# Twenty more weight pairs by seven half-size products in a hybrid mLSTM, GLA and SwiGLU block, with one weight sum made by an accumulating transfer

## The chip, the cores and the metric

The kernel is one program on one core of a Trainium2 chip. Its time is the device time of a launch in microseconds, the median of three runs. The work is shared by five engines with queues of their own, each in order: PE (TensorE, matrix products), ACT (ScalarE), DVE (VectorE), POOL (GpSimd) and SP (SyncE, which here only issues transfers). A queue stands still while its first instruction waits.

## The reference, cut to what matters

```python
for l in range(DEPTH):                       # DEPTH = 1, 512 tokens, 16 meta tokens, D_MODEL = 1024
    xn = rmsnorm(h, norm1_g[l])
    proj = jnp.where(valid, xn @ w_in[l].astype(dt), 0.0).astype(dt)
    (mq, mk, mv, mi, mf, mo, gq, gk, gv, ga, gr, gate_m, gate_g) = split_cols(proj)
    ...
    y_m = hm.reshape(bsz, tp, M_V).astype(dt)      # chunked mLSTM, 4 heads, head norm, gate sigmoid(mo)
    ...
    y_g = hg.reshape(bsz, tp, G_V).astype(dt)      # chunked gated linear attention (GLA), 4 heads, gate silu(gr)
    merged = (jax.nn.sigmoid(gate_m) * (y_m @ w_branch_m[l].astype(dt))
              + jax.nn.sigmoid(gate_g) * (y_g @ w_branch_g[l].astype(dt)))
    h = h + merged @ w_out[l].astype(dt)
    hn = rmsnorm(h, norm2_g[l])
    ff = jax.nn.silu(hn @ w_ff_gate[l].astype(dt)) * (hn @ w_ff_up[l].astype(dt))
    h = h + ff @ w_ff_down[l].astype(dt)
out = rmsnorm(h, final_g)
```

Everything is float32. The two mixers read the same normed input, so their projections (mq to gate_g) are products of one 1024-row activation with many 128-column blocks of weights.

## The kernel before

Activations lie transposed: a tile has 128 features on the partitions and up to 528 tokens (16 meta tokens and 512 real ones) along the columns. A **unit** is one block of weights of 128 output features, a tile `raw` of 128x1024 that holds eight 128x128 blocks, one for each k of the 1024 input features. Full float32 accuracy is had from rounded products: each operand is split in a high part (rounded to float32r) and a low part (the rest), and `mm3` (L194 to L200) issues three matmuls per k: high by high (L198), high by low (L199), low by high (L200). The weights are split on the chip: `whi` (L164) is a cast on ACT, `wlo` (L169) a subtraction on DVE.

A unit over the real tokens only (`unit_real`) is 8 k of three matmuls with 512 columns; one over all tokens (`unit_all`) is 8 k of three matmuls for each of two halves of 264 columns. The units run one after the other in a fixed order (`ORDER`): gates; four mLSTM heads (mq, mk, mv, mv, mo, mo); four GLA heads (gq, gk, gv, gv, gr, gr) with the merge gates gm and the branch products bm of the mLSTM output put in after heads 1 and 2; then gg 0 to 7, bg 0 to 7 (branch of the GLA output), out 0 to 7; 22 pairs fg, fu of the feed-forward layer; 22 units of its down projection. Below, mv6 is the unit ("mv", 6), and so on.

The last 17 of the 22 feed-forward pairs take a cheaper form already. Instead of two products over k = 0 to 7 with 512 columns, a **pair** is seven products over four k with 256 columns (a Strassen scheme): 7 x 4 x 3 = 84 matmuls, L1054 to L1056. The products are named p7, q1, p3, q6, p4, p2, q5; each takes one 128x512 sum of quarters of the two weight tiles and one sum of parts of the activations. The activation sums are made once (`operands`); the weight sums for each pair by four additions of 128x512 on DVE (L1014, L1015, L1018, L1021), and then split by ACT and DVE.

What sets the order around the change: while a unit u runs, `ahead` (L184) asks at k = 0 for the transfer of unit u + 5 (`load_raw`, SP's queue, four `raw` tiles), and at k = 2 and 4 splits the weights of unit u + 3. After each k, `tick` (L136) moves every side generator one step: evacuation of the products (`evac_all`, `evac_real`, `gates_of`), the convolution on mq and mk (`conv`, L451 and L454 on DVE), and, one head after the other, the mixers (`mlstm`, `gla`), whose rows are interleaved in this way into PE's, DVE's and ACT's queues. At the end of a head `head_out` norms its output and splits it into high and low parts (L570 on ACT, L572 on DVE) for the branch units.

## Time and profile before

| | |
|---|---|
| median of 3 runs | 956.32 us (956.04 to 956.37) |
| the profiled execution | 956.21 us, its span in the trace 954.2 us, mean granted TensorE clock 0.997 |
| transfers | 89.40 MB, mean 94 GB/s |

The span is the time from the first to the last instruction in the trace; about 2 us of the execution lie outside it. "Busy" counts an engine's instructions, not the waits between them. PE's matmuls overlap, so the time that one costs is the distance from its start to the start of the next, not its recorded duration; the same holds in a smaller measure on DVE and ACT, where a following instruction starts before the recorded end of the one ahead.

### The profile page before, as it was taken

The page shows a single profiled execution, that of the slowest core. Times are in us where ns is not written, and L with a number is a line of the kernel's source. Part 1 is how long each engine was busy: PE and PEld are TensorE (multiplying, and loading weights), DVE is VectorE, ACT ScalarE, POOL GpSimd, SP SyncE. Part 2 cuts the span into 40 slices and gives each one's busy share as a digit, 9 for nine tenths or more (in the row PEclk, how much of TensorE's full clock was granted, in tenths as well). Part 3 has the DMA queues.
Part 4 walks back from the last instruction along what each step waited for, and adds up shares of the span by engine and source line. Part 5 has one row for each costly group of instructions (what it writes and reads, how often), then busy time and mean ns, then how long its engine had stood idle before and what let it go on. Part 6 is the DMA issues. An engine that isn't in the chain of part 4 may idle for free.

```text
span 954.2 us, 13802 instructions
## 1 busy us (share of the span) xinstructions
PE 935.1 (98%) x5687; PEld 832.8 (87%) x5687; DVE 601.2 (63%) x876; ACT 467.6 (49%) x778; POOL 11.7 (1%) x30
## 2 busy tenths in 40 slices
PE   6999999999999999999999999999999999999995
PEld 6988989898988898889888888879999999888885
DVE  6898877674854543452354555798888887842323
ACT  7457667675552544262442234445555555732321
POOL 0000000000000000000000000010000000000000
PEclk9999999999999999999999999999999999999998
DMA  7322221212223232233223343223334233422202
GB/s 262 110 89 69 87 89 45 89 50 84 71 70 94 81 88 85 66 111 89 67 67 110 111 136 129 67 89 105 117 90 129 93 111 112 133 90 87 89 1 88
DMA packets 27294, 89.40 MB, mean 94 GB/s; under 512 B 3040, under 2 KB 5088, under 8 KB 27232
## 3 DMA queue, kind: packets, MB, share of 16 engines
q1 hardware_dynamic: 26144, 87.49, 29.2%
q10 hardware_dynamic: 1088, 1.05, 0.3%
q8 instruction: 44, 0.72, 0.3%
q14 instruction: 18, 0.15, 0.1%
HBM read 86.43 MB, written 2.10 MB: 93 GB/s over the span
## 4 chain that ended last, share of the span: by engine, by line
PE 88%; DVE 8%; ACT 2%; issue 1%; DMA 1%; SPq 0%; DVEq 0%
PE b L198 21%; PE b L200 21%; PE b L199 21%; PE b L1055 6%; PE b L1056 6%; PE b L1054 6%; DVE wlo L169 1%; PE b L767 1%; ACT t L116 1%; PE b L769 1%; PE b L746 1%; PE b L653 1%; PE b L486 1%; PE b L654 1%; DMA t<-xT 1%
## 5 line engine op out<-in xcount | busy, mean ns | idle before, releaser
L198 PE MATMUL b<-t,whi 128*128 128x512 f32 (+2 forms) x1222 | 434.9, 356 | 6.9 <-ACT t L116 6.9
L200 PE MATMUL b<-t,wlo 128*128 128x512 f32 (+2 forms) x1222 | 427.4, 350 | 0.7 <-DVE wlo L169 0.7
L199 PE MATMUL b<-t,whi 128*128 128x512 f32 (+2 forms) x1222 | 427.0, 349 | 0.7 <-DVE t L272 0.7
L198 PEld LDWEIGHTS b<-t,whi 128*128 128x128 f32 x1222 | 231.2, 189 | 36.2 <-ACT t L116 6.8
L200 PEld LDWEIGHTS b<-t,wlo 128*128 128x128 f32 x1222 | 230.8, 189 | 32.6 <-DVE wlo L169 1.1
L199 PEld LDWEIGHTS b<-t,whi 128*128 128x128 f32 x1222 | 231.3, 189 | 30.4 <-DVE t L272 1.0
L169 DVE TENSOR_TENSOR wlo<-raw,whi 128x1024 fp32r<-128x1024 f32 x138 | 168.2, 1223 | 96.0 <-ACT whi L164 95.9
L164 ACT CAST whi<-raw 128x1024 fp32r<-128x1024 f32 x138 | 142.9, 1047 | 17.7 <-issue 7.1
L1056 PE MATMUL b<-t,wlo 128*128 128x256 f32 x408 | 114.6, 281 | 0.0
L1055 PE MATMUL b<-t,whi 128*128 128x256 f32 x408 | 114.5, 281 | 0.0
L1054 PE MATMUL b<-t,whi 128*128 128x256 f32 x408 | 114.2, 280 | 0.0
L1054 PEld LDWEIGHTS b<-t,whi 128*128 128x128 f32 x408 | 76.9, 188 | 0.1
L1055 PEld LDWEIGHTS b<-t,whi 128*128 128x128 f32 x408 | 76.8, 188 | 0.1
L1056 PEld LDWEIGHTS b<-t,wlo 128*128 128x128 f32 x408 | 76.7, 188 | 0.0
L116 ACT ACTIVATE t<-t 128x512 f32<-128x512 f32 (+3 forms) x78 | 43.7, 579 | 45.0 <-DVE t L553 19.5
L116 ACT ACTIVATE t<-b 128x512 f32<-128x512 f32 (+1 forms) x65 | 33.5, 541 | 55.6 <-PE b L200 23.2
L169 DVE TENSOR_TENSOR wlo<-ws,whi 128x1024 fp32r<-128x1024 f32 x34 | 41.5, 1221 | 7.4 <-ACT whi L164 7.4
L116 ACT ACTIVATE t<-f 128x256 f32<-128x256 f32 (+1 forms) x24 | 11.6, 482 | 67.2 <-DVE f L1205 67.2
L1070 ACT COPY t<-b 128x256 f32<-128x256 f32 x51 | 19.0, 373 | 45.6 <-PE b L1056 45.6
L1205 DVE TENSOR_TENSOR f<-f,b 128x512 f32<-128x512 f32 (+1 forms) x9 | 5.7, 629 | 53.9 <-PE b L200 53.9
L164 ACT CAST whi<-ws 128x1024 fp32r<-128x1024 f32 x34 | 35.8, 1052 | 6.3 <-DVE ws L1021 3.5
L791 DVE TENSOR_TENSOR t<-b,t 128x512 f32<-128x512 f32 x16 | 11.1, 691 | 30.8 <-PE b L200 30.8
(200 smaller groups left out, 958.0 us busy)
## 6 DMA issues: line engine op xcount, KB each, us to landing
raw<-wst SPq DMA_DIRECT2D x155, 512.0 KB, 3.5
t<-xT SPq DMA_DIRECT2D x8, 264.0 KB, 5.6
t<-xT SPq DMA_DIRECT2D x8, 256.0 KB, 3.7
out<-t SPq DMA_DIRECT2D x4, 256.0 KB, 2.3
out<-t ACTq DMA_DIRECT2D x4, 256.0 KB, 2.5
cn<-con SPq DMA_DIRECT2D x1, 516.0 KB, 7.3
pr<-par SPq DMA_DIRECT2D x1, 320.0 KB, 7.1
pr<-par SPq DMA_DIRECT2D x1, 44.0 KB, 1.9
```

Source lines behind the costliest of these rows:

```text
L116: S.activation(o, i, func, **kw)
L164: S.copy(t, src)
L169: V.tensor_tensor(t, src, hi.bitcast(F32), ALU.subtract)
L198: T.matmul(o, w_h, ah[:, c0:c1], start=first, stop=False)
L199: T.matmul(o, w_h, al[:, c0:c1], start=False, stop=False)
L200: T.matmul(o, w_l, ah[:, c0:c1], start=False, stop=last)
L486: T.transpose(pb[:, c * P:(c + 1) * P], f[:, c * CH:(c + 1) * CH], ident)
L791: V.tensor_tensor(t, ps, t, ALU.mult)
L1054: T.matmul(o, h, xh_[k], start=start and k == 0, stop=False, skip_group_check=not start)
L1055: T.matmul(o, h, xl_[k], start=False, stop=False, skip_group_check=not start)
L1056: T.matmul(o, l, xh_[k], start=False, stop=k == 3, skip_group_check=not start)
L1070: s7=lambda: S.copy(s[:, lo], bz), s1=lambda: S.copy(s[:, hi], bx), s2=lambda: S.copy(r[:, lo], bx),
```

## The change

Twenty more pairs are run by seven half-size products: (gq, gk) and both gv and both gr of each GLA head, and gm and gg two by two. The pairs that need all tokens (gq with gk, gv) have 272 columns in each product, the others 256. The new generator `mixed_x` makes the seven sets of activation operands from the normed input while mv6, mv7, mo6 and mo7 run. It has 32 steps, and before the first gm pair the program issues all that is left of it (`while len(X.w["p4"][1]) < 4: tick()`). The order of the units changes (`JOBS`): after the mLSTM heads come gm0-1, gm2-3, GLA head 0, gm4-5, gm6-7, bm 0 to 7, the other heads with their parts interleaved, gg 0 to 7 between and behind them, bg 0 to 7.

Every pair, the 17 old ones too, now gets two of its four weight sums by accumulating transfers that POOL issues: one onto half of the second unit's `raw` tile (L182), one onto half of a tile `wf` that SP first fills (L210, L211), two pairs ahead of its use. DVE makes the other two (`s2` at L226, `s4` at L238). Weights are split two items ahead instead of three units, from four buffers instead of five. Several additions and multiplications move from DVE to ACT: the first tap of the convolution (L451 before, an activation now), two squares, a minimum in the GLA decay and a scaling of the GLA state. `head_out` no longer splits its result: `parts` does (L829 on ACT, L830 on DVE), just ahead of the first branch unit (bm0, bg0); only two tiles of the GLA output are split under gg6.

```diff
 NSTD = 5
...
+def job_list():
+
+    one = lambda *a: [(x,) for x in a]
+    o = one(("gates", 0))
     for h in range(H):
-        o += m(h)
-    for h in range(H):
-        o += g(h)
-        if h in (1, 2):
-            for i in range(4 * h - 4, 4 * h):
-                o += [("gm", i)] if i % 2 == 0 else [("gm", i), ("bm", i - 1), ("bm", i)]
-    o += [("gg", i) for i in range(8)] + [("bg", i) for i in range(8)]
+        o += one(("mq", h), ("mk", h), ("mv", 2 * h), ("mv", 2 * h + 1), ("mo", 2 * h), ("mo", 2 * h + 1))
+    two = lambda n, i: [((n, 2 * i), (n, 2 * i + 1))]
+    g = lambda h: [(("gq", h), ("gk", h))] + two("gv", h) + two("gr", h)
+    bm = lambda i: one(("bm", 2 * i), ("bm", 2 * i + 1))
+    o += two("gm", 0) + two("gm", 1) + g(0) + two("gm", 2) + two("gm", 3)
+    for i in range(4):
+        o += bm(i)
+    q, v, r = ([g(h)[i] for h in range(H)] for i in range(3))
+    o += [q[1], v[1], q[2], r[1], v[2], q[3], r[2], v[3]] + two("gg", 0) + [r[3]]
+    for i in range(1, 4):
+        o += two("gg", i)
+    for i in range(8):
+        o += one(("bg", i))
...
+            if v - 1 in MIXED:
+                G.dma_start(lr(r, 0), lr(wst[v - 1], 0), accum_op=ALU.add)
...
-        t = wpool.tile([P, D], F32R, tag="wlo", name=nm("wlo"), bufs=5)
+        t = wpool.tile([P, D], F32R, tag="wlo", name=nm("wlo"), bufs=4)
...
+            st.f = wpool.tile([P, D], F32, tag="wf", name=nm("wf"), bufs=2)
+            nc.sync.dma_start(lr(st.f, 1), lr(wst[u + 1], 0))
+            G.dma_start(lr(st.f, 1), lr(wst[u + 1], 1), accum_op=ALU.add)
...
+    def s2(u):
+        b = raws.pop(u + 1)
+        V.tensor_tensor(lr(mixw[u].f, 0), lr(b, 0), lr(b, 1), ALU.add)
...
+    PLAIN = {"s": [(split_hi, 2), (split_lo, 4)], "e": [(e_hi, 1), (e_lo, 3), (s2, 4)],
+             "a": [(a_hi, 1), (a_lo, 3), (f_hi, 4), (s4, 5)]}
+    FIRST = {"s": [(split_hi, ("q1", 2)), (split_lo, ("p3", 1))],
+             "e": [(e_hi, ("q1", 2)), (e_lo, ("p3", 1)), (s2, ("q6", 1))]}
+    SECOND = {"s": [(split_hi, ("p2", 0)), (split_lo, ("p2", 2))],
+              "a": [(a_hi, ("p2", 0)), (a_lo, ("p2", 2)), (f_hi, ("q5", 0)), (s4, ("q5", 2))],
+              "e": [(e_hi, ("p2", 0)), (e_lo, ("p2", 2)), (s2, ("q5", 2))]}
...
+        load_raw(u + 5)
+        while ready[0] < min(item_ix[0] + 2, len(ITEMS)):
+            kind, v = ITEMS[ready[0]]
+            ready[0] += 1
+            for f, at in tables.pop(0)[kind]:
+                steps.setdefault(at, []).append(lambda f=f, v=v: f(v))
...
+        seven(bz, w, x, "p7", True, hook, *cols)
+        seven(bx, w, x, "q1", True, hook, *cols)
+        if "p3" in pend:
+            pend.pop("p3")(hook)
+        else:
+            for k in range(4):
+                hook("p3", k)
+        seven(bx, w, x, "q6", False, hook, *cols)
+        seven(bz, w, x, "p4", False, hook, *cols)
+        seven(by, w, x, "p2", True, hook, *cols)
...
+        h, l = X.h, X.l
+        c1, c2 = slice(0, HA), slice(256, NT)
+        X.w = {n: ([], []) for n in SEVEN}
...
+        for k in (0, 2):
+            for j in range(2):
+                t = tt(F32R, 2 * HA)
+                for i in range(2):
+                    c = slice(i * HA, (i + 1) * HA)
+                    S.copy(t[:, c], (h, l)[j][k + i][:, c1])
+                    X.w["q1"][j].append(t[:, c])
+                yield 1
+            t1, t3 = tt(n=2 * HA), tt(n=2 * HA)
+            for j in range(2):
+                b1, b2 = tt(), tt()
+                u1, u3 = three(t1)[:, j], three(t3)[:, j]
+                V.tensor_tensor(b1, h[k + j].bitcast(F32), l[k + j].bitcast(F32), ALU.add)
+                yield 1
+                V.tensor_tensor(b2, h[k + 4 + j].bitcast(F32), l[k + 4 + j].bitcast(F32), ALU.add)
+                yield 1
+                V.tensor_tensor(u1, b1[:, c1], b1[:, c2], ALU.subtract)
+                V.tensor_tensor(u3, b2[:, c2], b1[:, c2], ALU.subtract)
+                yield 1
+                two("q5", u1, j)
+                yield 1
+                two("p7", u3, j)
+                V.tensor_tensor(u1, u1, b2[:, c2], ALU.add)
+                yield 1
+                two("q6", u1, j, True)
+                V.tensor_tensor(u3, u1, b2[:, c1], ALU.subtract)
+                yield 1
+                two("p4", u3, j)
...
+    def parts(y, k):
+
+        if k < 6 and y is ym:
+            hi = hpool[0].tile([P, NS], F32R, tag="h", name=nm("h"))
+        else:
+            hi = tt(F32R, NS)
+        lo = tt(F32R, NS)
+        S.copy(hi, y[k])
+        V.tensor_tensor(lo, y[k], hi.bitcast(F32), ALU.subtract)
+        y[k] = hi, lo
...
+    def joined(y, k):
+        while y[k] is None:
+            tick()
+        if not isinstance(y[k], tuple):
+            parts(y, k)
+
+    def branch_unit(name, y):
+        for k in range(KT):
+            joined(y, k)
+        return unit_real(name, [a[0] for a in y], [a[1] for a in y])
...
+            if what == "gm" and i == 0:
+                while len(X.w["p4"][1]) < 4:
+                    tick()
...
+            if i == 3:
+                run(mixed_x())
...
-            V.tensor_tensor(lr(st.s, 0), lr(st.b, 0), lr(st.a, 0), ALU.add)
-            V.tensor_tensor(lr(st.r, 0), lr(st.b, 0), lr(st.b, 1), ALU.add)
```

How the rows on the engines move, at three places. In DVE's queue of the kernel before, this stands around the weight split that is issued while mv6 runs, there that of mo7 (L617, L630 and L634 are the state chain of mLSTM head 3, L567 and L572 the output of head 2, L454 the convolution of head 3, L169 a weight split):

```order
L617 TENSOR_TENSOR t_1840<-b_1836,t_1840 128x400
L567 TENSOR_TENSOR t_1151<-t_1151,t_1687 128x512
L454 SCALAR_TENSOR_TENSOR t_1877<-t_1864,pr,t_1877 128x528
L169 TENSOR_TENSOR wlo_1916<-raw_1684,whi_1887 128x1024
L630 TENSOR_TENSOR wl_1784<-t_1840,wh_1783 128x400
L634 TENSOR_TENSOR t_1789<-t_1789,t_1840 128x400
L572 TENSOR_TENSOR t_1919<-t_1151,t_1918 128x512
L567 TENSOR_TENSOR t_1160<-t_1160,t_1687 128x512
L617 TENSOR_TENSOR t_1896<-b_1892,t_1896 128x272
L630 TENSOR_TENSOR wl_1784<-t_1896,wh_1783 128x272
```

In DVE's queue of the changed kernel, ahead of and behind the weight split issued while mv6 runs, now that of mo6 (L885, L898 and L902 are that state chain, L818 the output of head 2, L704 the convolution, L192 a weight split; L540 to L569 are `mixed_x`: sums and differences of activation tiles, and L569 the low part of each operand set, whose high part ACT has cast):

```order
L540 TENSOR_TENSOR t_1903<-t_566,t_567 128x528
L885 TENSOR_TENSOR t_1843<-b_1839,t_1843 128x400
L818 TENSOR_TENSOR t_1159<-t_1159,t_1688 128x512
L704 SCALAR_TENSOR_TENSOR t_1883<-t_1868,pr,t_1883 128x528
L542 TENSOR_TENSOR t_1904<-t_863,t_864 128x528
L192 TENSOR_TENSOR wlo_1931<-raw_1595,whi_1896 128x1024
L818 TENSOR_TENSOR t_1168<-t_1168,t_1688 128x512
L544 TENSOR_TENSOR t_1901<-t_1903 128x272
L545 TENSOR_TENSOR t_1902<-t_1904,t_1903 128x272
L569 TENSOR_TENSOR t_1943<-t_1901,t_1942 128x272
L898 TENSOR_TENSOR wl_1787<-t_1843,wh_1786 128x400
L902 TENSOR_TENSOR t_1792<-t_1792,t_1843 128x400
```

Of ten rows before, none made operands; of these twelve, five do (L540 to L569), and `mixed_x` has 40 such rows in all between the start of mv6 and the start of gm0-1.

In DVE's queue before, the end of the last GLA head's output, ahead of bg0 (L562, L563, L567 norm it, L572 splits its two tiles, L169 splits weights, L791 takes up the product of bg0):

```order
L562 TENSOR_SCALAR t_4629<-t_4629 128x512
L563 TENSOR_TENSOR t_4628<-t_4628,t_4629 128x512
L567 TENSOR_TENSOR t_4470<-t_4470,t_4628 128x512
L572 TENSOR_TENSOR t_4733<-t_4470,t_4732 128x512
L567 TENSOR_TENSOR t_4471<-t_4471,t_4628 128x512
L572 TENSOR_TENSOR t_4754<-t_4471,t_4753 128x512
L169 TENSOR_TENSOR wlo_4768<-raw_4659,whi_4759 128x1024
L169 TENSOR_TENSOR wlo_4799<-raw_4698,whi_4791 128x1024
L169 TENSOR_TENSOR wlo_4834<-raw_4742,whi_4826 128x1024
L791 TENSOR_TENSOR t_4565<-b_4810,t_4565 128x512
L793 TENSOR_TENSOR t_4565<-t_4565,t_3208 128x512
```

In DVE's queue of the changed kernel, at the end of the last gg pair and ahead of bg0 (L404 evacuates that pair, L830 splits tiles of the output, L803, L811, L812 and L818 norm the last head):

```order
L404 TENSOR_TENSOR t_5647<-b_5646,t_5649 128x256
L830 TENSOR_TENSOR t_5785<-h_4904,t_5784 128x512
L830 TENSOR_TENSOR t_5789<-h_4916,t_5788 128x512
L830 TENSOR_TENSOR t_5793<-h_5393,t_5792 128x512
L830 TENSOR_TENSOR t_5797<-h_5405,t_5796 128x512
L803 TENSOR_SCALAR t_5800<-b_5775 128x512
L811 SCALAR_TENSOR_TENSOR t_5659<-t_5659,t_5800 128x512
L812 SCALAR_TENSOR_TENSOR t_5658<-t_5659,t_5658 128x512
L818 TENSOR_TENSOR h_5808<-t_5158,t_5658 128x512
L830 TENSOR_TENSOR t_5811<-h_5808,t_5810 128x512
L818 TENSOR_TENSOR h_5814<-t_5159,t_5658 128x512
L830 TENSOR_TENSOR t_5817<-h_5814,t_5816 128x512
```

The split of the last two tiles stood three weight splits ahead of bg0's product; now nothing of another kind stands between it and the branch unit, and four splits of earlier heads stand ahead of the norm.

In POOL's queue before, between the last clearing of convolution edges (L444) and the products for the first feed-forward units (L949), nothing stood but two clears:

```order
L444 MEMSET t_1349 128x3
L444 MEMSET t_1768 128x3
L444 MEMSET t_1864 128x3
L674 MEMSET t_2191 128x512
L674 MEMSET t_2193 128x512
L949 ISA
L949 TENSOR_TENSOR t_5540<-t_5539,t_5540 128x512
```

In POOL's queue of the changed kernel, from the first accumulating transfer onto a `raw` tile on (L182 onto a `raw` tile, L211 onto `wf`, L853 the gate selector of a head, L695 clearing edges):

```order
L182 DMA raw_1858<-wst 128x512
L695 MEMSET t_1868 128x3
L182 DMA raw_2089<-wst 128x512
L853 CAST sel_2233<-cn 128x256
L182 DMA raw_2279<-wst 128x512
L211 DMA wf_2308<-wst 128x512
L182 DMA raw_2450<-wst 128x512
L211 DMA wf_2480<-wst 128x512
L182 DMA raw_2613<-wst 128x512
```

74 accumulating transfers are new in this queue, two for each of 37 pairs.

More of the change, by code (lines that the diff above doesn't have):

```diff
@@ L954, in hybrid_block @@
     xw = {}
+    hx = [[fpool.tile([P, 2, NS], F32, tag="hx", name=nm("hx"), bufs=2) for _ in range(2)] for _ in range(1)][0]
     def operands():
@@ L1190, in block @@
             held[u] = splits.pop(u)
+            down_steps["now"] = begin(("down", u - first))[1]
         mm3(o, held[u], flat % KT, fsp[k][0], fsp[k][1], c0, c1, k == 0, k == FT - 1)
         if prefetch:
-            ahead(u, flat % KT)
+            for f in down_steps["now"].get(flat % KT, ()):
+                f()
         tick()
```

536 lines of the change are left out of this document (299 added, 237 removed).

## The prediction

> **What bounds the kernel now.** I read the page's busy times first, then the chain that ended last, then what PE waited for.
>
> ```profile
> span 954.2 us, 13802 instructions
> ...
> PE 935.1 (98%) x5687; PEld 832.8 (87%) x5687; DVE 601.2 (63%) x876; ACT 467.6 (49%) x778; POOL 11.7 (1%) x30
> ...
> PE 88%; DVE 8%; ACT 2%; issue 1%; DMA 1%; SPq 0%; DVEq 0%
> ```
>
> ```profile
> PE b L198 <- ACT t L116: 6.9, 1, 6.9
> PE b L610 <- DVE t L495: 1.1, 1, 1.1
> PE b L1231 <- ACT t L116: 1.0, 1, 1.0
> ```
>
> PE is busy for 98% of the span and makes up 88% of the chain. Its longest wait is the first 6.9 us; the other two are about 1 us. So what PE executes is the time, as long as DVE and ACT keep ahead of it. The change cuts PE's work and gives DVE more, so I need PE's saving and then the places where DVE falls behind.
>
> **PE's saving.** Recorded durations overlap, so I take distances from start to start in a gapless row of matmuls.
>
> ```profile
> 23.26 0.28 PE L199 MATMUL b<-t,whi 128*128 128x264 f32 x1
> ...
> 24.84 0.28 PE L200 MATMUL b<-t,wlo 128*128 128x264 f32 x1
> ```
>
> ```profile
> 178.20 0.29 PE L652 MATMUL b<-wh,t 128*128 128x272 f32 x1
> ...
> 178.58 0.23 PE L652 MATMUL b<-wh,t 128*128 128x144 f32 x1
> ```
>
> ```profile
> 300.36 0.39 PE L199 MATMUL b<-t,whi 128*128 128x512 f32 x1
> ...
> 301.52 0.40 PE L198 MATMUL b<-t,whi 128*128 128x512 f32 x1
> ```
>
> With 264 columns: 13 steps in 1.58 us, 0.1215 each. With 272: three in 0.38, 0.127; scaled from 264 it would be 0.125, I take 0.126. With 512: five in 1.16, 0.232. For 256 the stretch of the old pairs serves, 651 to 815 us (next fence): 164.0 us for 1391 matmuls, 0.118.
>
> ```profile
> 8.00:24.50 16.50, 16.34 (x111) 16.22 (x112) 14.96 (x19) 14.51 (x24) 1.09 (x2) 1.00 0.67 266
> ...
> 651.00:815.00 164.00, 164.00 (x1391) 163.96 (x1390) 138.37 (x196) 95.00 (x168) 1.61 (x1) 1.00 0.35 107
> ```
>
> Removed: 28 units over real tokens (4 gq, 8 gr, 8 gm, 8 gg) x 24 = 672 matmuls of 512, 155.9 us; 12 over all tokens (4 gk, 8 gv) x 48 = 576 of 264, 70.0 us. Added: 12 pairs x 84 = 1008 of 256, 118.9 us; 8 pairs x 84 = 672 of 272, 84.7 us. Net: 225.9 - 203.6 = **22.3 us less** (21.7 with 0.127, 23 with 0.125). Bounded by PE alone, the profiled execution of 956.2 us would come to 933.9.
>
> **What DVE gets, and where.** These rows show what DVE instructions cost back to back, which is some 0.08 us less than their recorded time.
>
> ```profile
> 163.08 0.77 DVE L454 SCALAR_TENSOR_TENSOR t<-t,pr,t 128x528 f32<-128x528 f32 x1
> 163.75 0.57 DVE L617 TENSOR_TENSOR t<-b,t 128x400 f32<-128x400 f32 x1
> 164.24 0.69 DVE L567 TENSOR_TENSOR t<-t,t 128x512 f32<-128x512 f32 x1
> ...
> 171.84 0.43 DVE L634 TENSOR_TENSOR t<-t,t 128x272 f32<-128x272 f32 x1
> 172.19 0.69 DVE L572 TENSOR_TENSOR t<-t,t 128x512 fp32r<-128x512 f32 x1
> 172.80 0.69 DVE L470 TENSOR_TENSOR t<-t,t 128x512 fp32r<-128x512 f32 x1
> 173.40 0.30 DVE L617 TENSOR_TENSOR t<-b,t 128x144 f32<-128x144 f32 x1
> 173.62 0.70 DVE L470 TENSOR_TENSOR t<-t,t 128x528 fp32r<-128x528 f32 x1
> 174.23 0.30 DVE L630 TENSOR_TENSOR wl<-t,wh 128x144 fp32r<-128x144 f32 x1
> ...
> 174.67 1.22 DVE L169 TENSOR_TENSOR wlo<-raw,whi 128x1024 fp32r<-128x1024 f32 x1
> 175.81 0.17 DVE L617 TENSOR_TENSOR t<-b,t 128x16 f32<-128x16 f32 x1
> ```
>
> So: 1024 columns 1.13, 528 0.61 (scalar-tensor-tensor 0.67), 512 0.60, 400 0.49, 272 0.36, 144 0.22, 16 0.09.
>
> The steady pair is fine. It needs three weight splits (3.4), one low part, two sums (three of 512, 1.8) and four evacuations of 256 to 272 (1.4): 6.6 us of DVE beside 9.9 to 10.6 us of PE. The 17 old pairs lose two sums each, 1.2 us of DVE, and gain nothing: PE is gapless there, 164.00 of 164.00.
>
> The heavy place is **mixed_x under mv6, mv7, mo6, mo7**. Its own 40 DVE instructions are 8 of 528 and 32 of 272, 8 x 0.61 + 32 x 0.37 (four are scalar-tensor-tensor) = 16.6 us. Counting DVE's queue in its new order from the first row behind mv6's first matmul (a convolution tap) up to the low weights that the pair gm0-1 needs for q6: 76 instructions, 5 of 1024, 12 of 528 (three of them taps), 15 of 512, 35 of 272, 3 each of 400, 144 and 16, together 37.6 us. PE's own work from mv6's first matmul to that product is 33.9 us. Up to the same product of (gq0, gk0) it is 117 instructions, 60.3 us, against 56.0 us of PE. So DVE's work exceeds PE's by 4.3 us; and since PE cannot start q6 before it, that excess is a stall. After this the next pairs leave room (one pair on, in gv0, it is 71 against 71).
>
> Two things come on top. The first of those DVE rows cannot run at mv6's start: ACT must copy both halves of mk3 (0.375 each) and make the first tap, which is now an activation of 528 (0.64).
>
> ```profile
> L326 ACT COPY t<-b 128x264 f32<-128x264 f32 x38 | 13.1, 375 | 24.3 <-PE b L200 24.3
> L116 ACT ACTIVATE t<-t 128x528 f32<-128x528 f32 x21 | 12.7, 636 | 4.4 <-DVE t L454 4.3
> ```
>
> That is 1.4 us, or 2.5 with one weight cast between, which I take. And DVE waits for ACT inside: every operand set is cast on ACT before DVE can make its low part. In the same stretch before, 158 to 188 us, such waits are these:
>
> ```profile
> 158.00:188.00 30.00, 30.00 (x196) 27.36 (x195) 22.67 (x39) 18.39 (x37) 1.05 (x2) 1.00 0.23 79
> ```
>
> ```profile
> L495 DVE TENSOR_TENSOR t<-b,t 128x512 fp32r<-128x512 f32 x2 | 1.4, 692 | 3.0 <-ACT t L490 3.0
> ...
> L630 DVE TENSOR_TENSOR wl<-t,wh 128x272 fp32r<-128x272 f32 x1 | 0.4, 443 | 2.2 <-ACT wh L621 2.2
> ```
>
> DVE idles 7.3 of 30 us there, without being late. With a full queue part of it is filled: I take 7% of 60 us, 4.2. The stall is 4.3 + 2.5 + 4.2 = **11 us**, between 4 (the excess alone) and 17 (ACT as slow as in the row, 9 us of waits).
>
> **The ends of the mixers.** Before, the last GLA head was split three units ahead of bg0. Now, as DVE's queue shows, the last head's norm stands behind four splits. From the end of the gg6 pair: those four end some 1.5 us later (4 x 0.60, begun when the pair's evacuation at q5 is done); then L803 0.6, three activations on ACT, two scalar-tensor-tensor 0.67 each, the product 0.6, the cast, the low part 0.6.
>
> ```profile
> L116 ACT ACTIVATE t<-t 128x512 f32<-128x512 f32 x34 | 21.1, 626 | 32.0 <-DVE t L553 19.5 <-DVE t L944 7.1 <-DVE t L454 3.3
> ```
>
> With 0.6 for each on ACT, k = 6 is ready 7.4 us after the pair's end, k = 7 at 9.4. PE comes to k = 6 at 6 x 0.70 + 1.4 (the p3 still owed) = 5.6 us, and would end the unit at 7.0; it ends near 9.9, and eight handings from engine to engine add about half a microsecond: **3.5 us** (2 to 6). At bm0 eight splits stand just ahead, at 0.60 each against 0.70 of PE per k; only the first is late: **1 us** (0 to 2). The rest of GLA's rows, now closer together: **1 us** (0 to 3). The early stretch gets taps on ACT and may lose half of the 1.1 us at L610: **-0.7**.
>
> **The transfers.** Each pair adds three of 128x512, 0.79 MB; 29 MB in all. The fence above shows 266 GB/s in the first stretch and 107 under the old pairs, so there is room. A plain load lands in 3.5 us:
>
> ```profile
> raw<-wst SPq DMA_DIRECT2D x155, 512.0 KB, 3.5
> ```
>
> No accumulating transfer, and none from POOL, is in this trace. A `raw` tile is asked for more than a pair (some 12 us) before its split, so up to 8 us for the accumulation cost nothing. I take nothing, between 0 and the case below. The Trainium skill ("DMA: Bandwidth & Descriptors", Anatomy of one DMA) gives 2.0 us plus bytes over 436e3 for a transfer issued by GpSimd, an estimate of 2.6 us for 256 KB; no run here shows it, and the sum would stay as it is. What stands behind a waiting accumulation in POOL's queue are other accumulations, a head's selector and, in the feed-forward part, its products for the standard units.
>
> **Sum.** 956.2 - 22.3 + 11 + 3.5 + 1 + 1 - 0.7 = **949.7 us** for the profiled execution, which lies 0.1 under the median.
>
> **The rivals.** (1) PE stays the bound: DVE's rows with no bond to PE run ahead of where they are issued, the stretch costs 2 us instead of 11, the ends 1: about 936. For it speaks that DVE is at 63%; against it the excess of 4.3 us in the count, which no order can hide.
>
> (2) A cold clock. At the start PE ran at half pace after its first idle time:
>
> ```profile
> 8.15 0.59 PE L199 MATMUL b<-t,whi 128*128 128x264 f32 x1 [0.71 <-DVE t L272]
> ...
> 13.38 0.39 PE L198 MATMUL b<-t,whi 128*128 128x264 f32 x1
> 13.60 0.29 PE L199 MATMUL b<-t,whi 128*128 128x264 f32 x1
> 13.73 0.28 PE L200 MATMUL b<-t,wlo 128*128 128x264 f32 x1
> ```
>
> Steps of 0.22 (13.38 to 13.60) up to 13.6, then 0.12: 5.4 us at about half pace, 2.4 lost. If the stall at gm0-1 comes in one piece and another such follows, that price is paid twice: 954.5. No wait in the middle of this trace is over 1.3 us, so it is neither shown nor excluded. The Trainium skill ("TensorE: Matmul & The Clock Gate", Part 1) says that the clock falls to half after an idle window of about 3.4 us and returns after about as long of sustained work; by that rule this rival decides whenever a single wait passes 3.4 us, and the slow start agrees with it in kind, though its 5.4 us are longer.
>
> (3) Slower: the exchange between DVE and ACT in mixed_x. There are 16 casts whose low part stands next in DVE's queue. If each costs 1 us of waiting (as in the two rows above, 1.5 and 2.2 each), the waits are 16 us instead of 4.2 and the total 961.5. It turns slower than before at 10.7 us of waits.
>
> (4) Slower by transfers: an accumulation of over 8 us comes late in each of 37 pairs; at 9 us, 37 us are lost, some 987. Nothing in the trace speaks for it.
>
> **How the numbers follow.** Forecast 949.7 (943 to 954): 0.52. PE bound: 0.17. Cold clock: 0.12. Exchange: 0.14. Transfers: 0.05. A measurement tells about 0.2% from no change, so the bounds are 954.4 and 958.2. Faster: 0.50 + 0.17 + half of the cold clock = 0.73. Same: the other half, 0.02 of the forecast and 0.02 of the exchange, 0.10. Slower: 0.17. The range 934 to 962 leaves out about 0.06 below and 0.12 above.
>
> **What would show it.** PE's matmuls of 256 and 272 columns at 0.118 and 0.126 apart; PE's waits by the list: one group of about 11 us between mv6 and the second pair, ended by DVE rows of mixed_x or a weight split; one of 3.5 us in bg0, ended by the split L830 or L829; none in the old pairs. The prediction is wrong if PE waits for a transfer, if those waits are missing, or if steps of 0.22 show up behind a wait.

## The result and the profile after

The changed kernel takes **986.3 us** (median of four runs, 985.17 to 988.49), the kernel before 956.35 us beside it (four runs, 956.04 to 956.56): a ratio of 1.0316 with an interval of 1.0298 to 1.0334. The forecast was 949.7 us with a range up to 962. The profiled execution took 985.17 us, its span 983.4, at a mean granted clock of 0.979 (0.997 before).

The page of the changed kernel: span, busy times, the granted clock in 40 slices of 24.6 us, and the chain that ended last by engine.

```profile
span 983.4 us, 15554 instructions
...
PE 925.5 (94%) x6119; PEld 848.8 (86%) x6119; DVE 651.0 (66%) x970; ACT 551.6 (56%) x959; POOL 78.5 (8%) x107
...
PEclk9999999879999999999997999999999999999998
...
PE 78%; DVE 11%; ACT 9%; issue 2%; DMA 0%; SPq 0%; DVEq 0%; ACTq 0%
```

PE's share of the chain fell from 88% to 78%, and DVE and ACT took it, not a transfer. The clock has a dent in three slices inside (172 to 221 and 516 to 541 us), those of PE's longest waits; the dent in the last slice was there before. PE's waits in the changed kernel (what PE executes, what ended the wait; us in all, times, longest):

```profile
PE b L340 <- ACT t L402: 9.0, 2, 8.4
PE b L300 <- DVE wlo L192: 7.5, 4, 3.6
PE b L340 <- ACT t L400: 7.4, 5, 4.4
PE b L298 <- ACT t L132: 6.7, 1, 6.7
PE b L736 <- ACT t L579: 6.4, 1, 6.4
PE b L340 <- ACT t L568: 4.4, 1, 4.4
```

The 6.7 is the start, as before. The others are new, and most of them end at ACT, where the prediction looked at DVE.

To see where the time went I worked through all of PE's matmul starts. A distance from one start to the next that exceeds its kind's spacing (0.232 for 512 columns, 0.1215 for 264, 0.126 for 272, 0.118 for 256) by more than 0.45 us counts as a wait, with its excess; smaller excesses over 0.05 us count as slow matmuls, added up in slices of 5 us where they pass 0.5.

| place (us of the changed span) | waits | slow matmuls | together | prediction |
|---|---|---|---|---|
| mv6 to gq0 and what follows, 174 to 260 | 20.7 | 6.7 | 27.4 | 11 |
| bg0, 516 to 530 | 8.6 | 1.9 | 10.5 | 3.5 |
| early units, 46 to 65 | 4.2 | 0.9 | 5.1 | -0.7 |
| standard feed-forward units, 644 to 660 | 6.3 | 1.4 | 7.7 | 0 |
| the rest (301 to 512, and 682) | 4.3 | 0 | 4.3 | 2 |

Together 55.0 us, against 2.9 in the middle of the kernel before (2.1 at 55 to 72 us, 0.85 at 634): 52.1 more. The spans differ by 29.2 us (983.4 - 954.2), so what is neither wait nor slow matmul fell by 52.1 - 29.2 = 22.9 us. The count of matmuls at the same spacings (672 fewer of 512 columns, 576 fewer of 264, 1008 more of 256, 672 more of 272) gives 22.3. So the saving is there, and new waits take it back more than twice. Of the 10.9 us of slow matmuls 9.4 stand behind the five waits of 3.8 us and more; the 0.9 at 60 us and the 0.6 at 190 us stand where the granted clock is 1.00, so they are not the clock's doing.

Where nothing waits the change does what it says. One window of the changed kernel under the old pairs (busy us and instructions of PE, PEld, DVE, ACT, POOL; granted clock; share of the DMA engines; GB/s), and the one over mixed_x:

```profile
690.00:850.00 160.00, 160.00 (x1348) 159.74 (x1347) 116.36 (x163) 91.30 (x163) 24.38 (x28) 1.00 0.74 178
158.00:217.00 59.00, 42.67 (x249) 37.54 (x248) 45.06 (x86) 38.77 (x84) 3.97 (x6) 0.87 0.28 68
```

Under the old pairs PE is gapless with the DMA engines busy 0.74 of the time. Over mixed_x PE is busy for 42.67 of 59 us; the kernel before has 59.00 in the same window, with 44.16 us of DVE.

### The profile page after: what moved, and what is told of

It reads as the page before. It is cut to its first block, busy times and chain, and to the rows that moved or that the text cites. A ratio compares the mean times of both kernels' runs of the same rounds, so it can differ in the third digit from the quotient of the medians.

```text
span 983.4 us, 15554 instructions
## 1 busy us (share of the span) xinstructions
PE 925.5 (94%) x6119; PEld 848.8 (86%) x6119; DVE 651.0 (66%) x970; ACT 551.6 (56%) x959; POOL 78.5 (8%) x107
## 4 chain that ended last, share of the span: by engine, by line
PE 78%; DVE 11%; ACT 9%; issue 2%; DMA 0%; SPq 0%; DVEq 0%; ACTq 0%
PE b L298 13%; PE b L300 13%; PE b L299 13%; PE b L340 11%; PE b L341 11%; PE b L342 11%; ACT t L132 4%; DVE wlo L192 2%; ACT whi L187 1%; PE b L1037 1%; ACT L132 1%; ACT L130 1%; PE b L1039 1%; DVE t L830 1%; PE b L736 1%
## 5 line engine op out<-in xcount | busy, mean ns | idle before, releaser
L299 PE MATMUL b<-t,whi 128*128 128x512 f32 (+2 forms) x806 | 284.6, 353 | 1.0 <-DVE t L467 0.7
L298 PE MATMUL b<-t,whi 128*128 128x512 f32 (+2 forms) x758 | 269.2, 355 | 8.6 <-ACT t L132 6.7
L300 PE MATMUL b<-t,wlo 128*128 128x512 f32 (+2 forms) x758 | 266.2, 351 | 7.5 <-DVE wlo L192 7.5
L340 PE MATMUL b<-t,whi 128*128 128x256 f32 (+1 forms) x888 | 258.3, 291 | 14.3 <-ACT t L400 7.4
L341 PE MATMUL b<-t,whi 128*128 128x256 f32 (+1 forms) x888 | 252.4, 284 | 0.7 <-DVE t L569 0.7
L342 PE MATMUL b<-t,wlo 128*128 128x256 f32 (+1 forms) x888 | 252.1, 284 | 0.0
L192 DVE TENSOR_TENSOR wlo<-raw,whi 128x1024 fp32r<-128x1024 f32 x155 | 189.6, 1227 | 54.0 <-ACT whi L187 53.9
L132 ACT ACTIVATE t<-t 128x512 f32<-128x512 f32 (+4 forms) x118 | 67.2, 589 | 26.9 <-DVE t L646 6.8
L182 POOL DMA_DIRECT2D raw<-wst x37 | 32.1, 867 | 411.0 <-DMA wf<-wst 95.0
L187 ACT CAST whi<-wf 128x1024 fp32r<-128x1024 f32 x37 | 38.9, 1051 | 24.0 <-PE b L341 16.5
L340 PE MATMUL b<-t,wgh 128*128 128x256 f32 (+1 forms) x148 | 42.6, 288 | 9.0 <-ACT t L402 9.0
L192 DVE TENSOR_TENSOR wlo<-wf,whi 128x1024 fp32r<-128x1024 f32 x37 | 45.1, 1219 | 0.0
L341 PE MATMUL b<-t,wgh 128*128 128x256 f32 (+1 forms) x148 | 42.4, 286 | 0.0
L342 PE MATMUL b<-t,wgl 128*128 128x256 f32 (+1 forms) x148 | 42.4, 286 | 0.0
```

The costliest lines, as they stand in the source:

```text
L132: S.activation(o, i, func, **kw)
L182: G.dma_start(lr(r, 0), lr(wst[v - 1], 0), accum_op=ALU.add)
L187: S.copy(t, src)
L192: V.tensor_tensor(t, src, hi.bitcast(F32), ALU.subtract)
L298: T.matmul(o, w_h, ah[:, c0:c1], start=first, stop=False)
L299: T.matmul(o, w_h, al[:, c0:c1], start=False, stop=False)
```

## The experiments

Fifteen kernels were run, each beside the kernel before, whose medians lay between 956.2 and 956.4 us. The numbers given are medians of three to five runs (ten for the last version), with the interval of the ratio where the verdict hangs on it. The line numbers in a profile are those of that kernel and shift by a few.

### The lead of the weight splits

The waits at 46 to 55 us and 644 to 660 us lie in units that the change does not touch, but for their weights' split, now two items ahead. In the first kernel that lead is three again wherever four standard units follow each other.

```diff
-        tables = [PLAIN] if len(names) == 1 else [FIRST, SECOND]
+        tables = [PLAIN, PLAIN] if len(names) == 1 else [FIRST, SECOND]
+        far = 3 if all(len(x) == 1 for x in JOBS[j:j + 4]) else 2
...
-        while ready[0] < min(item_ix[0] + 2, len(ITEMS)):
+        while ready[0] < min(item_ix[0] + far, len(ITEMS)):
```

> Weights of single units are split three units ahead again where the next three are single units too; the pairs stay at two items. Theory: the waits at 46 to 55 us (4.2 us) and at 644 to 652 us (6.3 us), with the half-speed matmuls behind them (2.3 us), come from the shorter lead, since DVE and ACT are held up there by other chains that the kernel before has too. They go: 973 to 976 us. Rival, DVE has too much work there: the waits stay, 984 to 987. The waits between mv6 and the first pairs and the one in bg0 stay in both.

Measured: 976.79 us, 9.5 less. Both groups of waits are gone but for 0.9 us at 653.8; three others (0.85, 1.65 and 1.65) appear between 67 and 102 us.

The counterpart shortens the lead in the kernel before, of the single units ahead of the pairs, and changes nothing else.

```diff
-        if not SW0 <= u + 3 < SW1:
+        n = 3 if u >= SW1 else 2
+        if not SW0 <= u + n < SW1:
...
-                split_hi(u + 3)
+                split_hi(u + n)
...
-                split_lo(u + 3)
+                split_lo(u + n)
```

> The kernel before, with the weights of single units ahead of the pairs split two units ahead and not three. Theory: the lead of three is what hides the gate rows at 40 to 60 us and the operands of the feed-forward pairs at 600 to 645 us; without it PE waits there as in the changed kernel, 4 and 6 us and some slow matmuls: 964 to 969 us. Rival: the changed kernel's waits there come from what it moved to ACT: 956 to 958.

Measured: 968.66 us, a ratio of 1.0126 (1.0109 to 1.0143), 12.4 us slower than before. PE's waits in that kernel:

```profile
PE b L201 <- DVE wlo L169: 7.1, 3, 3.6
PE b L199 <- ACT t L116: 6.8, 1, 6.8
PE b L199 <- ACT whi L164: 1.9, 2, 1.3
```

They are 1.42 and 2.18 us at 52 to 56 us, then 1.56, 0.85 and 3.79 at 626 to 638, the sizes that the changed kernel has (1.44 and 2.19, then 1.62, 0.85 and 3.79). So the lead alone makes them; neither pairs nor transfers are needed. Why the first group comes there, ACT's timeline of the changed kernel shows (start, us, instruction, in brackets its wait):

```profile
50.67 0.63 ACT L132 ACTIVATE t<-t 32x512 fp32r<-32x512 f32 x1 [6.78 <-DVE t L646]
51.86 0.62 ACT L656 CAST t<-t 32x512 fp32r<-32x512 f32 x1 [0.55 <-DVE t L653]
52.51 0.62 ACT L658 COPY t<-t 32x512 f32<-32x512 f32 x1
53.15 1.04 ACT L187 CAST whi<-raw 128x1024 fp32r<-128x1024 f32 x1
```

ACT waits 6.78 us for the gate rows on DVE, and the weight cast stands behind. The kernel before has the same wait, of 6.80 us at 50.39, and PE does not notice: the weights in question were split one unit earlier. In the second group DVE is full: it is busy for 13.45 of the 13.6 us from 642.6 to 656.2, and the low parts of the weights stand in its queue among the operand sums of the old pairs (L1265 to L1296). The lead is what covers such chains and such a crowd.

### bg0: a copy behind the last head's norm

PE's longest new wait ends at L402, a copy of one quarter of the last gg pair (s5). It is issued after k = 0 of bg0, behind everything that makes bg0's operands. ACT and PE of the changed kernel there:

```profile
515.86 1.28 ACT L130 ACT_TABLE_LOAD   x1
518.39 1.95 ACT L132 ACTIVATE t<-t 128x512 f32<-128x512 f32 x3 [1.25 <-DVE t L803]
522.55 0.62 ACT L829 CAST t<-h 128x512 fp32r<-128x512 f32 x1 [2.21 <-DVE h L818]
524.53 0.62 ACT L829 CAST t<-h 128x512 fp32r<-128x512 f32 x1 [1.36 <-DVE h L818]
525.05 0.36 ACT L402 COPY t<-b 128x256 f32<-128x256 f32 x1
```

```profile
516.69 0.40 PE L300 MATMUL b<-t,wlo 128*128 128x512 f32 x1
525.47 0.58 PE L340 MATMUL b<-t,wgh 128*128 128x256 f32 x1 [8.38 <-ACT t L402]
525.85 0.42 PE L341 MATMUL b<-t,wgh 128*128 128x256 f32 x1
526.07 0.42 PE L342 MATMUL b<-t,wgl 128*128 128x256 f32 x1
...
529.05 0.59 PE L300 MATMUL b<-t,wlo 128*128 128x512 f32 x1
529.48 0.39 PE L298 MATMUL b<-t,whi 128*128 128x512 f32 x1
529.71 0.40 PE L299 MATMUL b<-t,whi 128*128 128x512 f32 x1
```

The pair's owed product p3 (wgh) accumulates into the bank that L402 reads, so after k = 2 PE stands there, not at k = 6. In the second kernel the copy is issued ahead of the two last tiles' chain.

```diff
         for k in range(KT):
+            if k == 6:
+                left("s5")
             joined(y, k)
```

> In the first branch unit of each mixer the copy that the owed product p3 waits for is issued ahead of the last head's norm and not behind it. Theory: PE's wait of 8.6 us in bg0 is that copy standing in ACT's queue behind the norm; with the copy first 3 to 4 us are left, at k = 6 and 7, and the clock stays up: 978 to 981 us. Rival, the norm itself is what PE waits for: 984 to 987.

Measured: 980.58 us, 5.7 less (4.3 by the profiled executions, 985.17 and 980.89). The copy runs at 515.75, and PE now waits at k = 6 and 7: 2.79, 0.49, 0.68 and 0.49 us, 4.5 in all, with 1.6 us of slow matmuls behind. The 4.5 is the wait that the prediction described, and near its 3.5.

### mixed_x

Two kernels take it away or move its casts. In the first the operand sets are not made: views of the split normed input stand in for five of the seven, so the twenty new pairs compute another result.

```diff
+        for n in ("q1", "q5", "q6", "p4", "p7"):
+            for k in range(4):
+                for j in range(2):
+                    X.w[n][j].append((h, l)[j][k][:, c1])
+        yield 31
```

> mixed_x makes no operands (its additions, subtractions, casts and low parts are left out, views of the normed input stand in their place); everything else, the pairs too, is as in the changed kernel. Theory: the waits from 174 to 260 us (19.7 us) and the slow matmuls behind them (6.7 us) are its exchange between DVE and ACT: 958 to 966 us. Rival, the accumulating transfers or the pairs' own splits hold PE there: 980 to 986.

Measured: 968.13 us, 18.2 less. That is a little above the 958 to 966 expected. Waits of 0.6 and 2.9 us are left of the first two of the stretch (6.6 and 4.6), and PE is busy for 54.74 us of the window 158 to 217 instead of 42.67. So two thirds of the 27.4 us are mixed_x's work; the rest is what else changed there.

In the second, DVE makes the high parts too, so that no low part waits for ACT, and DVE has some 5 us more to do.

```diff
-            act(hi, src, AF.Copy, scale=-1.0)
+            V.tensor_scalar(hi, src, -1.0, None, op0=ALU.mult)
...
-            S.copy(hi, src)
+            V.tensor_copy(hi, src)
```

> The changed kernel, with the 16 high parts of mixed_x made by DVE and not by ACT: 4 to 5 us more work on DVE, but no low part there waits for ACT any more. Theory: the stretch is slow by the exchange between the two queues and not by the amount of work, so PE's waits from 174 to 212 us shrink: 975 to 981 us. Rival, the amount of DVE's work decides: the waits grow by the 4 to 5 us: 988 to 992.

Measured: 984.84 us (1.0280 to 1.0314), no clear difference from the changed kernel. The long waits of the stretch are 3.6, 1.4, 5.8 and 5.3 us instead of 6.6, 4.6, 1.2 and 4.8. So neither the queue's length nor the exchange explains the stretch alone: easing one at the price of the other gains nothing that the intervals tell apart. The changed kernel's own timeline shows both. DVE, then ACT, then PE:

```profile
165.78 0.77 DVE L704 SCALAR_TENSOR_TENSOR t<-t,pr,t 128x528 f32<-128x528 f32 x1 [4.50 <-ACT t L132]
...
177.52 0.44 DVE L569 TENSOR_TENSOR t<-t,t 128x272 fp32r<-128x272 f32 x1 [1.37 <-ACT t L568]
...
180.07 0.44 DVE L566 SCALAR_TENSOR_TENSOR t<-t,t 128x272 fp32r<-128x272 f32 x1 [1.41 <-ACT t L132]
```

```profile
174.28 0.42 ACT L568 CAST t<-t 128x272 fp32r<-128x272 f32 x1 [2.90 <-DVE t L544]
174.72 1.28 ACT L132 ACT_TABLE_LOAD   x1
...
177.50 1.28 ACT L130 ACT_TABLE_LOAD   x1
...
181.22 0.65 ACT L579 COPY t<-b 128x264 f32<-128x264 f32 x2
```

```profile
174.81 0.40 PE L300 MATMUL b<-t,wlo 128*128 128x512 f32 x1
181.65 1.11 PE L736 MATMUL b<-pr,t 128*128 128x128 f32 x4 [6.44 <-ACT t L579]
```

The waits run in both directions: DVE waits for ACT's tap (4.50) and casts (1.37, 1.41), ACT waits for DVE's sums (2.90) and reloads its function table twice (1.28 each). PE's first long wait is not for an operand of a pair at all, but for the copy of a finished mv unit (L579) that stands in ACT's queue behind those casts. Of the 59 us of the window, DVE is idle for 13.9 (59.00 - 45.06), and all its waits of more than a moment end at ACT. The longest is the one for the tap, and nine are for casts of mixed_x (what DVE executes, what ended the wait; us in all, times, longest):

```profile
DVE t L704 <- ACT t L132: 4.5, 1, 4.5
DVE t L569 <- ACT t L568: 3.4, 6, 1.4
DVE t L566 <- ACT t L132: 2.5, 3, 1.4
```

Two groups of 1.4 and 1.1 us follow, 12.9 in all. ACT in turn waits 20.1 us for DVE in the window. In the kernel before, DVE idles there as long (59.00 - 44.16 = 14.8 us) and PE waits for nothing; idle time of DVE is a loss only where something that PE needs soon stands behind it.

### Moving mixed_x ahead

If the stretch is only too dense, the steps of mixed_x can be spread from head 2 on, one every third tick (all its yields, of which one is shown).

```diff
-            yield 1
+            yield 3
...
-            if i == 3:
+            if i == 2:
```

> mixed_x starts one mLSTM head earlier and takes a step at every third tick, so that its DVE and ACT work is spread over some 90 us instead of 28. Theory: its cost of 18.6 us (with no operands made: 966.5 in the profiled execution) is crowding, so most of it goes: 968 to 974 us. Rival: the work itself is too much wherever it stands, or its waits hit other chains: 980 us or more.

Measured: 987.08 us (1.0302 to 1.0344), no gain, where 968 to 974 was expected. A count may explain a part: 32 steps of three ticks are 96, and only 80 ticks lie between there and the first gm pair, so the last five or so steps were still issued at once ahead of it. That this alone undid the gain is not shown. Together with the first two edits:

> The lead of three for single units, the copy ahead of the norm and the early, slow mixed_x together. Theory: the three causes are independent, so their gains add: 986.3 - 9.5 - 5.7 - (gain of the early mixed_x, 12 to 18): 953 to 960 us. Rival: they share waits, and the total stays over 963.

Measured: 972.97 us, which is what those two give (986.3 - 9.5 - 5.7 = 971.1); a miss against 953 to 960. On top of this, two variants. One issues the high parts of the next weights later in a pair, at p3 instead of q1:

```diff
-    FIRST = {"s": [(split_hi, ("q1", 2)), (split_lo, ("p3", 1))],
-             "e": [(e_hi, ("q1", 2)), (e_lo, ("p3", 1)), (s2, ("q6", 1))]}
+    FIRST = {"s": [(split_hi, ("p3", 0)), (split_lo, ("p3", 3))],
+             "e": [(e_hi, ("p3", 0)), (e_lo, ("p3", 3)), (s2, ("q6", 1))]}
```

> As with the three together, and in a pair the cast of the next pair's second unit stands behind the copies s1 and s7 in ACT's queue, not ahead. Theory: PE's waits of 0.6 to 1.3 us at q6 in the new pairs (eight or so, 7 us) are the copy behind that 1.05 us cast; they go: 5 to 7 us less than with the three alone. Rival: ACT is behind for other reasons: no change.

Measured: 971.17 us, 1.8 less where 5 to 7 were expected; the intervals (1.0159 to 1.0199 and 1.0139 to 1.0178) overlap. The other moves the side generators on at every k of a pair instead of every second:

```diff
-            if k % 2:
-                tick()
+            tick()
```

> As with the three together, and a pair steps the side work at each k, 28 times, not 14. Theory: the last GLA head's norm is late in bg0 because a pair gives 14 steps where two units gave 16 and the order has shortened its time; with 28 the norm ends before bg0 and its remaining waits (4.5 us) go: 4 to 5 us less than with the three alone. Rival: closer steps crowd ACT and DVE and the new pairs wait more: slower than the three.

Measured: 991.12 us, 18 slower. The wait in bg0 shrinks to 1.35 us, but waits of some 3 us come up at 312, 368 and 436 us. At 368 and 436 activations of the mixers, now issued earlier, stand ahead of the pair's own copy (L400); at 312 PE waits for the operand casts of bm0 (L829).

The next three versions build on the kernel with the later high parts. In the first, gm0 to gm3 are single units again, so that mixed_x has more room (32 steps from head 3 on, every second tick); in the second, besides, the last head's gates gr come ahead of gg0; in the third, on top of both, the gg pairs tick at every k, and the last quarter of mixed_x steps at every tick.

```diff
-    o += two("gm", 0) + two("gm", 1) + g(0) + two("gm", 2) + two("gm", 3)
+    o += one(*(("gm", i) for i in range(4))) + g(0) + two("gm", 2) + two("gm", 3)
```

> As with the cast behind the copies (971.2 us), but mixed_x starts where the changed kernel starts it and takes a step at every second tick, and gm 0 to 3 run as single units ahead of the first pair, so that 8 units (51 us) and not 4 cover it; two pairs fewer cost PE 2.4 us. Theory: the 16 us of waits and 4 to 5 us of slow matmuls between 174 and 220 us go down to 4: 956 to 961 us. Rival: the waits only move behind the four units: 968 or more.

> As the one before, with the last gr pair ahead of gg0-1, so that the last GLA head's norm has one more pair (10 us) before bg0. Theory: the waits in bg0 (4.3 us) and the slow matmuls there (1.7 us) go: 5 to 6 us less than without it. Rival: the head's chain is bound to the steps of its generator and ends as late: no change.

> As the one with the last gr pair ahead of gg0-1, but the gg pairs step the side work at each k, and the last quarter of mixed_x takes every step. Theory: the wait in bg0 is set by the number of steps that the last GLA head gets, so with gg pairs at 28 steps the norm is done before bg0 (4.5 us of waits and 2 of slow matmuls go), and the wait of 4.5 us at the first pair for mixed_x's last casts goes as well: 950 to 954 us, under the kernel before. Rival: closer steps in the gg pairs only make waits there: 960 or more.

Measured: 962.44 us, a little above the 956 to 961 expected (a wait of 4.4 us for an operand cast is left at the first pair; the single units and the pace of mixed_x change together here, and no run separates them); 963.27, no change; and 959.60 (1.0022 to 1.0049), less gained than the 950 to 954 expected, though the wait in bg0 is gone. Two waits of 2.6 us remain at the first pair.

The last version also gives the first tap of the convolution back to DVE, for which DVE waited 4.50 us above.

```diff
-        act(a, raw[:, 3 + c0:3 + c0 + n], AF.Identity, scale=pr[:, col + 3:col + 4], bias=pr[:, C_CB + m:C_CB + m + 1])
+        V.tensor_scalar(a, raw[:, 3 + c0:3 + c0 + n], pr[:, col + 3:col + 4], pr[:, C_CB + m:C_CB + m + 1],
+                        op0=ALU.mult, op1=ALU.add)
```

> As the one with gg pairs at 28 steps (959.6 us), with the first tap of the convolution on DVE again. Theory: that tap in ACT's queue makes DVE wait for ACT ahead of each convolution and is what is left of the early waits (67 to 102 us, 4.2 us) and of those from 174 to 196 (3.6 us): 953 to 957 us. Rival: DVE is the fuller queue there and loses 0.4 to 0.5 us for each of 8 taps: 960 to 963.

Measured: **955.19 us** over ten runs, a ratio of 0.9990 (0.9980 to 0.9999): 4.4 us less than without the edit, as expected. The waits from 67 to 104 us fall from 4.2 us to 1.7, those from 176 to 196 from 3.6 to 0.8. Beside the kernel before it is level: the interval ends just below 1, but 0.1% is less than such a measurement tells. Its page and waits:

```profile
span 953.5 us, 15357 instructions
...
PE 920.8 (97%) x6047; PEld 841.5 (88%) x6047; DVE 645.4 (68%) x964; ACT 534.8 (56%) x935; POOL 74.7 (8%) x103
```

```profile
PE b L343 <- DVE wlo L192: 3.5, 4, 1.5
PE b L341 <- ACT whi L187: 3.0, 2, 2.3
PE b L341 <- ACT t L569: 2.4, 1, 2.4
```

By the same reckoning, start and end included, 19.4 us of waits and 7.0 of slow matmuls are left (4.4 and 3.3 before). Four single gm units are 96 x 0.232 = 22.3 us, as two pairs 168 x 0.118 = 19.8; so 2.5 of the 22.3 us saved by the count are given up, and the other 19.8 pay for 18.7 more of waits and slow matmuls and little else.

### The weight sums by transfers

The rival on late transfers had 37 us. In this kernel the two sums of each pair are made by DVE instead, and the 74 accumulating transfers and 37 plain ones are gone.

```diff
-                G.dma_start(lr(r, 0), lr(wst[v - 1], 0), accum_op=ALU.add)
...
-            nc.sync.dma_start(lr(st.f, 1), lr(wst[u + 1], 0))
-            G.dma_start(lr(st.f, 1), lr(wst[u + 1], 1), accum_op=ALU.add)
...
+        V.tensor_tensor(lr(mixw[u].f, 1), lr(b, 0), lr(b, 1), ALU.add)
+        V.tensor_tensor(lr(b, 0), lr(b, 0), lr(a, 0), ALU.add)
```

> The two weight sums are made by DVE again, for all 37 pairs, with no accumulating transfer. Theory: the transfers are hidden, so nothing is won; in the crowded stretch DVE gets 1.2 us more for each pair: 985 to 991 us. Rival, the accumulations come late or slow DVE or ACT down: under 980.

Measured: 1033.66 us, 47 slower than the changed kernel, where 985 to 991 was expected. The waits of its PE:

```profile
PE b L339 <- ACT t L399: 29.6, 15, 6.6
PE b L339 <- ACT t L1312: 11.0, 16, 3.0
```

The rival falls: in the changed kernel no wait of PE ends at a transfer, the longest wait of ACT for one (8.0 us at 669) has none of PE's behind it, and the transfers do not slow the other engines' instructions (a weight split on DVE takes 1222 ns in the median in both kernels, its cast on ACT 1049 before and 1047 after). The miss in size comes from the same oversight as elsewhere in this case. I had counted the additions as time of DVE; but the weight cast on ACT now waits for them, and the copies that free the banks (L399, and L1312 in the old pairs) stand behind that cast. Of ACT's waits in this kernel:

```profile
ACT whi L185 <- DVE raw L216: 50.4, 18, 9.8
```

DVE has room as a whole (126.75 us busy in a window of 160 over the old pairs), and PE still waits. The sums stand right ahead of the cast in this kernel, and no run makes them earlier; so the 47 us are the price of this place, and what well placed sums on DVE would cost is not shown.

### The clock behind a wait

Behind the wait in bg0 the matmuls are slow: the rows above show 0.21 to 0.22 us for 256 columns and 0.43 for 512, until 529.48, then 0.23. Is that the wait's doing, or the product's? This kernel fills the wait with 60 matmuls of 256 columns whose result nobody reads.

```diff
+            if name == ("bg", 0) and k == 2:
+                d = bank()
+                for i in range(60):
+                    T.matmul(d[:, :256], w[0][:, :P], ah[0][:, :256], start=i == 0, stop=i == 59)
```

> The changed kernel with 60 matmuls of 256 columns, their result unused, put into bg0 ahead of the owed product p3, where PE waits 8.6 us. Theory: they fill 7.1 us of that wait and no more, so the wait's end stays where it is, and the clock does not fall: the matmuls behind it come 0.118 and 0.232 apart at once and 1.5 to 2 us are saved: 984 to 985 us. Rival, the slow matmuls have nothing to do with the wait: they stay at 0.21 and 0.42 apart and the time at 986.3.

Measured: 983.67 us (1.0275 to 1.0321), an interval that overlaps the changed kernel's; the span is 1.6 us shorter. The rows decide here, PE of this kernel:

```profile
516.90 7.35 PE L314 MATMUL b<-t,whi 128*128 128x256 f32 x60
525.47 0.39 PE L344 MATMUL b<-t,wgh 128*128 128x256 f32 x1 [1.22 <-ACT t L406]
525.70 0.28 PE L345 MATMUL b<-t,wgh 128*128 128x256 f32 x1
```

p3 begins at 525.47, to the hundredth as without the filling, and its matmuls last 0.28 us instead of 0.42. The granted clock decides too (the last number but two), over the same 4 us in the changed kernel and in this one:

```profile
525.40:529.40 4.00, 3.93 (x15) 3.72 (x16) 2.03 (x3) 1.91 (x4) 0.00 (x0) 0.50 0.21 34
525.40:529.40 4.00, 3.93 (x23) 3.49 (x24) 2.03 (x3) 3.15 (x5) 0.00 (x0) 1.00 0.23 49
```

So PE's idle time makes the slow matmuls, some 1.9 us here.

## Why the prediction was wrong, step by step

- **PE's saving** (22.3 us) was right: the count stands, and the spans leave 22.9. So was **"the 17 old pairs gain nothing"**: gapless, 160.00 of 160.00.
- **The transfers at nothing** was right: no wait of PE ends at a DMA.
- **The stretch under mv6 to mo7** (11 us, bounds 4 to 17) is the largest error: 27.4. The step that failed is the term for DVE's waits for ACT: "7% of 60 us, 4.2", with 2.5 for the start, 6.7 together. Measured were 12.9 in 59 us, 4.5 of them for the tap at the start, and DVE was idle for 13.9 in all. The row it was taken from had 7.3 of 30 us (24%); I cut it to 7% on the ground that a full queue fills the gaps, but a queue in order fills nothing while its first instruction waits. 24% of 59 would have been 14.4. With 12.9 for the 6.7 the prediction's own sum is 4.3 + 12.9 = 17.2, and PE's waits up to 217 us are 17.2 (6.60, 4.56, 1.17, 4.82); no run confirms the 4.3 by itself. The rest of the 27.4 is 3.5 us in three waits for copies at 232 to 261, and 6.7 of slow matmuls. The rival on the exchange named the mechanism in one direction; the other, ACT waiting for DVE with the copies of finished units behind it, stood nowhere. How the 27.4 us divide between excess and exchange the runs don't settle: the casts on DVE traded one for the other at no gain.
- **The end at bg0** (3.5): 10.5. The chain was described rightly and is 4.5 once the copy is moved (the second kernel); the step missed that p3's copy is queued behind that chain. I counted p3 among PE's work ("the p3 still owed", 1.4 us) and not what it waits for. Moving the copy gave 5.7 us back.
- **"Early -0.7"** and nothing for the standard feed-forward units: 5.1 and 7.7. The shorter lead was named in the change and priced nowhere. Restoring the old lead gives 9.5 us back, and the short one alone costs the kernel before 12.4. The wait of 1.1 us at L610 is gone, as "-0.7" had it, but by luck: with the old lead restored (the first kernel) that instruction, L879 there, waits 1.49, longer than before, and in the kernel before with the short lead it does not wait either, though no tap has moved. PE has lost some 4 us to the new waits ahead of it by then, which would explain it.
- **bm0** at 1 was fair in size: waits of 0.46 and 0.77 us stand at 301 to 305. But the longer ends at the copy for an owed p3 (L402) and not at a split.
- **The cold clock** was a rival of its own with 0.12, as if it were another way to go. It follows from the waits: 9.4 us of slow matmuls behind five of them. Any forecast with a long wait in it should have carried this price; the steps of 0.21 and 0.43 behind waits are a sign that the prediction itself named for being wrong. The rule that the prediction cites from the Trainium skill ("TensorE: Matmul & The Clock Gate", Part 1) agrees with the waits of 3.8 us and more here. Shorter ones, of 2.2 and 2.6 us, were enough in other runs, as the last section shows.
- **Two slips in its counts** change nothing: a new pair has three evacuations on DVE, not four, and k = 7, ready at 9.4, ends the unit at 10.1 and not at 9.9.

Put right from the runs: 956.2 - 22.3 + 52.1 = 986.0, beside 985.17 for the profiled execution.

## What to carry to other kernels

How far ahead an operand is made is a price like an instruction's: look for the longest wait on the engines that make it, and see whether the lead still covers it. For each product count what it waits for by the whole queue in front of that instruction, evacuation copies too, and take the idle share of the nearest row as it is: here 24% before and 24% after, with more work in the queue. And a saving on the engine that bounds is spent as soon as two others must take turns for it: the best version here keeps 19.8 us of saved PE work and ends level with the kernel before.

## What the runs showed of the hardware

- **The clock falls in the middle of a kernel.** After waits of 3.8 to 8.6 us matmuls run at about half pace for some 3 us and more (525.47 to 529.48: 0.21 for 256 columns, 0.43 for 512, granted clock 0.50), which costs between 1.1 and 2.6 us each time. After single waits of 1.0 to 1.3 us (that begin at 230.8, 236.7 and 259.7) the granted clock is 1.00. Between these it depends: a wait of 2.18 us that ends at 56.1 in the kernel before with the short lead is followed by a granted clock of 0.50 (56.8 to 60.2), the same wait of 2.19 in the changed kernel by 1.00. In the last version a wait of 2.6 us that ends at 220.87 was enough, with smaller ones of 0.8 and 0.9 us ahead of it: the mean granted clock is 0.60 already while PE waits, and 0.50 behind. Together with a second wait of 2.6 us it cost 2.4 us of slow matmuls. The two stretches:

```profile
218.30:220.80 2.50, 0.17 (x2) 0.00 (x0) 2.21 (x6) 1.03 (x3) 0.00 (x0) 0.60 0.27 26
220.80:222.10 1.30, 1.23 (x3) 0.79 (x3) 1.23 (x4) 0.44 (x2) 0.00 (x0) 0.50 0.80 318
```

- **Accumulating transfers issued by POOL** landed in 4.8 and 5.5 us in the median, beside 3.5 us before for a plain load of twice the size and 3.3 for the plain load of the same size onto `wf`. Asked for two pairs ahead, they cost PE no wait. The rows give what is moved, the queue, the count, the size of one, and the median us from issue to landing, in the changed kernel:

```profile
wf<-wst POOLq DMA_DIRECT2D x37, 256.0 KB, 5.5
raw<-wst POOLq DMA_DIRECT2D x37, 256.0 KB, 4.8
```
